# Attention products of a hybrid decoder layer in two float32r parts instead of float32

## The chip, the cores and the metric

The kernel runs on one core of one Trainium2 chip. The metric is the device time of one execution in microseconds (us), here the median of several. In the profile PE is the matrix engine's products, PEld its weight loads, DVE the vector engine, ACT the scalar engine, POOL the GpSimd engine and SP the queue that issues most DMAs.

## The reference, cut to what matters

One decoder layer on 256 tokens, with 16 meta tokens in front (272 positions) and a model width of 2048. A combined input projection feeds two kinds of heads: 8 retention heads (`RH`) and 4 mLSTM heads (`MH`). Their outputs pass a head norm and a gate, then an output projection, then a convolution and a gated feed-forward part of width 5632. The part that is changed here is what each head does between the projections:

```python
# retention, per head and chunk
scores = einsum('bhncd,bhnsd->bhncs', q, k) * decay
intra  = einsum('bhncs,bhnse->bhnce', scores, v)
...
# mLSTM, per head and chunk
P   = einsum('bhncd,bhnsd->bhncs', q, k) * exp(D - m_t[..., None])
num = einsum('bhncs,bhnse->bhnce', P, v) + ...
den = sum(P, axis=-1) + ...
return num / maximum(abs(den), exp(-m_t))[..., None]
```

The recurrence over chunks is exact algebra for one causal attention over all 272 positions, and the kernel computes it in that form.

## The kernel before, in words

Positions lie on the columns. `T` = 272 is the number of positions, `NQ` = 258 the number of query positions that are needed. All large products (input projection `wi`, output projection `wo`, feed-forward `wu` and `wd`) take both operands in two float32r parts, a high part (the value rounded to float32r) and a low part (what is left), and add three products: high by high, high by low, low by high. `load_w` (L123 to L132) loads a half tile of weights, 128x1024, into `wraw`, ACT casts it to `whi` (L129) and DVE subtracts to get `wlo` (L131); there are four `wraw` and five `whi` and `wlo` buffers. `mmk` (L134) issues 16 products with `whi` (L138 with the high part of the activations, L139 with the low part) and then 8 with `wlo` (L141). `project` makes one 128-column tile of a projection out of two half tiles and leaves it in one of four PSUM buffers `mmps`.

The attention of a head has these steps, all in plain float32 on PE:

- `values` (L314) transposes the values on PE (L324), subtracts their mean and writes them to `vpad` in three blocks of key positions (L333, ACT).
- `scores` (L336 on) makes three products, one for each block of 128, 128 and 16 keys: the 258, 144 and 16 queries that see them (L339, L340, L341), weights from `kpad`.
- The scores are multiplied into `ppad` (DVE), and `weigh` (L344 on) makes three products with `vpad` as weights (L347, L348, L349). A retention head weighs once, an mLSTM head twice.
- An mLSTM head also needs row sums: POOL adds the second and third block into `late` (L464, L465), and two products with a matrix of ones add over the keys (L467, L468).
- `variance` (L351 on) makes the head norm: ACT squares and casts, DVE subtracts, two products add up (L359, L360), and `rsqrt_m2` (L160 on) goes over ACT (L164, L165, L167) and DVE (L168, L169). `put_mix` (L363) writes the result to `mixh` and `mixl`.

The loop at L491 projects head i and then attends head i-1, so that one head's attention runs beside the next head's projection. The last retention head's attention runs beside the output projection (L537 on), which starts on the heads that are done: for the first four output tiles the mLSTM half of the weights goes first, and the products that need the last head (`mixh[:, 7]`) come at the end. The order of instructions on each engine is set by a scheduler that places them by its own estimate of times; engines then run them strictly in that order.

At the start, `rstd1` (the first norm) is computed beside the first projections: ACT squares the inputs (L246), DVE adds them (L249, L254), one product adds over the partitions (L256), and `rsqrt_m2` and L258 follow. Until `rstd1` is there no projection tile can leave its PSUM buffer, since each is scaled by it: L420 and L416 (`cx`) are the first to do so. The gates of the mLSTM heads (L274 to L305) are short chains over ACT and DVE on 4 rows, and three small products (L301 to L303) turn one of them, `rA`, into columns.

## Time and profile before

| what | value |
|---|---|
| median of 3 runs | 1242.2 us (1242.07 to 1242.63) |
| time of the profiled execution | 1242.43 us |
| its span (first to last instruction) | 1240.7 us |
| PE busy | 1228.6 us, 99% |
| DVE busy | 810.6 us, 65% |
| ACT busy | 661.1 us, 53% |
| POOL busy | 64.5 us, 5% |
| HBM read | 220.75 MB, 180 GB/s over the span |

A float32 product appears in the trace as two instructions on PE, so a group of 16 such products has a count of 32; a float32r product is one. "Mean ns of one" of a PE instruction runs from its start until its result is out, and overlaps the next one; the distance from start to start is what it costs the engine.

### The profile page before, as it was taken

The numbers are of one execution on the slowest core, as the hardware profiler recorded it, in microseconds if no ns is written. First come the engines' busy times: TensorE is split into PE (matmuls) and PEld (weight loads), VectorE is DVE, ScalarE is ACT, GpSimd is POOL, SyncE is SP. The second block draws the span as 40 slices with busy tenths as digits, with TensorE's granted clock in tenths as the row PEclk, the third lists the DMA queues.
The fourth block names the chain that finished last, engine by engine and source line by source line (L and its number), as shares of the span: only waits on it lengthen the run. The fifth ranks groups of instructions, "written<-read, shape, count | busy, mean of one in ns | idle before, by whom it ended". The sixth has DMA issues, their size and how long they took to land.

```text
span 1240.7 us, 22240 instructions
## 1 busy us (share of the span) xinstructions
PE 1228.6 (99%) x9094; PEld 1176.9 (95%) x9094; DVE 810.6 (65%) x1188; ACT 661.1 (53%) x888; POOL 64.5 (5%) x72
## 2 busy tenths in 40 slices
PE   9999999999999999999999999999999999999996
PEld 9999999999999999999999998888999999998885
DVE  8867777766665766667767664445677677664452
ACT  8756756555556556555555543334555555554441
POOL 0100011111110110000000000000000000000010
PEclk9999999999999999999999999999999999999999
DMA  8764555555553666565555666666665555666552
GB/s 272 253 185 154 160 154 161 176 169 162 175 177 121 220 179 214 165 180 183 186 185 175 186 186 186 186 188 188 185 186 174 186 186 181 182 182 188 186 203 68
DMA packets 63687, 224.30 MB, mean 181 GB/s; under 512 B 7392, under 2 KB 8288, under 8 KB 63456
## 3 DMA queue, kind: packets, MB, share of 16 engines
q1 hardware_dynamic: 62928, 220.11, 57.2%
q0 software_dynamic: 656, 2.76, 0.7%
q8 instruction: 71, 1.16, 0.4%
q14 instruction: 32, 0.26, 0.1%
HBM read 220.75 MB, written 2.10 MB: 180 GB/s over the span
## 4 chain that ended last, share of the span: by engine, by line
PE 97%; DVE 1%; ACT 1%; DMA 1%; issue 0%; SPq 0%; ACTq 0%; DVEq 0%
PE mmps L138 24%; PE mmps L139 24%; PE mmps L141 24%; PE atps L630 7%; PE atps L633 7%; PE atps L629 7%; PE atps L347 1%; PE atps L339 0%; DMA wraw<-in_wi 0%; PE atps L324 0%; DMA hT<-in_xT 0%; PE atps L348 0%; DVE wlo L131 0%; PE atps L569 0%; PE atps L340 0%
## 5 line engine op out<-in xcount | busy, mean ns | idle before, releaser
L129 ACT CAST whi<-wraw 128x1024 fp32r<-128x1024 f32 x404 | 423.1, 1049 | 476.3 <-PE mmps L139 258.0
L131 DVE TENSOR_TENSOR wlo<-wraw,whi 128x1024 fp32r<-128x1024 f32 x404 | 495.2, 1227 | 198.7 <-ACT whi L129 191.2
L139 PE MATMUL mmps<-ul,whi 128*128 128x258 f32 x1408 | 345.8, 283 | 0.0
L138 PE MATMUL mmps<-uh,whi 128*128 128x258 f32 x1408 | 345.7, 282 | 0.0
L138 PEld LDWEIGHTS mmps<-uh,whi 128*128 128x128 f32 x1408 | 266.1, 189 | 0.1
L139 PEld LDWEIGHTS mmps<-ul,whi 128*128 128x128 f32 x1408 | 265.2, 188 | 0.1
L138 PE MATMUL mmps<-xh,whi 128*128 128x272 f32 (+2 forms) x880 | 223.5, 287 | 0.6 <-DVE cx L416 0.6
L139 PE MATMUL mmps<-xl,whi 128*128 128x272 f32 (+2 forms) x880 | 223.2, 287 | 0.0
L141 PE MATMUL mmps<-uh,wlo 128*128 128x258 f32 x1408 | 199.2, 284 | 0.0
L141 PEld LDWEIGHTS mmps<-uh,wlo 128*128 128x128 f32 x1408 | 182.4, 189 | 0.0
L138 PEld LDWEIGHTS mmps<-xh,whi 128*128 128x128 f32 x880 | 165.7, 188 | 0.8 <-ACT whi L129 0.8
L139 PEld LDWEIGHTS mmps<-xl,whi 128*128 128x128 f32 x880 | 166.0, 189 | 0.0
L630 PE MATMUL atps<-whi,ml 128*128 128x512 f32 x352 | 140.0, 398 | 0.0
L629 PE MATMUL atps<-whi,mh 128*128 128x512 f32 x352 | 138.1, 392 | 0.0
L141 PE MATMUL mmps<-xh,wlo 128*128 128x272 f32 (+2 forms) x880 | 129.1, 285 | 0.0
L141 PEld LDWEIGHTS mmps<-xh,wlo 128*128 128x128 f32 x880 | 116.4, 188 | 0.1
L574 DVE TENSOR_TENSOR cu<-mmps,rstd 128x258 f32<-128x258 f32 x88 | 37.5, 426 | 116.3 <-PE mmps L141 116.2
L633 PE MATMUL atps<-wlo,mh 128*128 128x512 f32 x352 | 110.4, 395 | 0.0
L630 PEld LDWEIGHTS atps<-whi,ml 128*128 128x128 f32 x352 | 66.1, 188 | 17.1
L633 PEld LDWEIGHTS atps<-wlo,mh 128*128 128x128 f32 x352 | 66.1, 188 | 15.9
L629 PEld LDWEIGHTS atps<-whi,mh 128*128 128x128 f32 x352 | 66.1, 188 | 14.9
L139 PE MATMUL mmps<-mixl,whi 128*128 128x258 f32 x256 | 63.1, 283 | 0.0
(210 smaller groups left out, 1026.3 us busy)
## 6 DMA issues: line engine op xcount, KB each, us to landing
wraw<-in_wu SPq DMA_DIRECT2D x176, 512.0 KB, 3.5
...
```

The lines of the kernel that those rows point to most:

```text
L129: nc.scalar.copy(hi, raw)
L131: nc.vector.tensor_tensor(out=lo, in0=raw, in1=hi.bitcast(F32), op=ALU.subtract)
L138: nc.tensor.matmul(ps, hi[:, k, :], xh(kk), start=kk == first, stop=False)
L139: nc.tensor.matmul(ps, hi[:, k, :], xl(kk), start=False, stop=False)
L141: nc.tensor.matmul(ps, lo[:, k, :], xh(kk), start=False, stop=kk == last)
L347: nc.tensor.matmul(ps[:, 0:NQ], lhs(0), pT[:, 0:CA], start=True, stop=False)
L574: nc.vector.tensor_tensor(out=u, in0=ps[:, :NQ], in1=rstd2, op=ALU.mult)
L629: nc.tensor.matmul(ps, mh[:, k, rows], hi[:, i, :], start=k == 0, stop=False)
L630: nc.tensor.matmul(ps, ml[:, k, rows], hi[:, i, :], start=False, stop=False)
L633: nc.tensor.matmul(ps, mh[:, k, rows], lo[:, i, :], start=False, stop=k == NHF - 1)
```

## The change

Keys, queries, values and weights of the attention are each split into a high and a low float32r part (`khl`, `vhl`, `phl` and two tiles `qh`, `ql`), by an ACT copy and a DVE subtraction each. `scores` and `weigh` then make three products for each of the three blocks, nine where there were three. The row sums of the mLSTM heads are made by `weigh` with a float32r matrix of ones (`ones_r`), two products a block, six where there were two and two additions on POOL. The pieces of 16 rows that were handled apart are now part of one instruction each. To make room, the squares of the first norm are taken in eight pieces of two instead of four pieces of four (`sum2`), and the gate rows use buffers of `wk`.

```diff
-    kpad = [pa.tile([P, 3 * P], F32, name=f"kpad{i}") for i in range(2)]
-    vpad = pa.tile([P, 3, 2 * P], F32, name="vpad")
-    ppad = pa.tile([P, ABC], F32, name="ppad")
...
+    khl = [[pa.tile([P, 3 * P], F32R, name=f"k{p}{i}") for p in "hl"] for i in range(2)]
+    vhl = [pa.tile([P, 3, 2 * P], F32R, name=f"v{p}") for p in "hl"]
+    phl = [pa.tile([P, ABC], F32R, name=f"p{p}") for p in "hl"]
...
-        sum4 = None
-        for k in range(0, KT, 4):
-
-            sq = rope if k % 8 else sqp.tile([P, 4, T], F32, name="sq" if k else "sum4")
+        sum2 = sqp.tile([P, 2, T], F32, name="sum2")
+        for k in range(0, KT, 2):
+
+            sq = rope[:, k % 4 : k % 4 + 2, :] if k else sum2
             with tc.issue_after(copied.ins):
-                squared = nc.scalar.activation(sq, hT[:, k : k + 4, :], AF.Square)
+                squared = nc.scalar.activation(sq, hT[:, k : k + 2, :], AF.Square)
             if k:
                 with tc.issue_after(parted.ins), tc.high_priority():
-                    nc.vector.tensor_tensor(out=sum4, in0=sum4, in1=sq, op=ALU.add)
...
+                    nc.vector.tensor_tensor(out=sum2, in0=sum2, in1=sq, op=ALU.add)
...
-            nc.tensor.matmul(ms[:, :T], inv_dm, sum4[:, 0, :], start=True, stop=True)
+            nc.tensor.matmul(ms[:, :T], inv_dm, sum2[:, 0, :], start=True, stop=True)
...
+            m = nm[0:n, b : b + 1]
+            nc.scalar.activation(vh[0:n, b, :], where[b], AF.Identity, bias=m)
+            nc.vector.scalar_tensor_tensor(out=vl[0:n, b, :], in0=where[b], scalar=m, in1=vh[0:n, b, :].bitcast(F32), op0=ALU.add, op1=ALU.subtract)
+        return vh, vl
+
+    def split(parts, x):
+        hi, lo = parts
+        nc.scalar.copy(hi, x)
+        nc.vector.tensor_tensor(out=lo, in0=x, in1=hi.bitcast(F32), op=ALU.subtract)
+        return parts
+
+
+    PAIRS = ((0, 0), (0, 1), (1, 0))
+
+    BLOCKS = ((0, 0, CA), (P - T0, CA, AB), (2 * P - T0, AB, ABC))
+
+    def scores(k, q):
 
         ps = at.tile([P, 512], F32, name="atps")
-        nc.tensor.matmul(ps[:, 0:CA], kT[:, 0:P], qT[:, 0:NQ], start=True, stop=True)
-        nc.tensor.matmul(ps[:, CA:AB], kT[:, P : 2 * P], qT[:, P - T0 : NQ], start=True, stop=True)
-        nc.tensor.matmul(ps[:, AB:ABC], kT[:, 2 * P : 3 * P], qT[:, 2 * P - T0 : NQ], start=True, stop=True)
+        for b, (c0, a0, a1) in enumerate(BLOCKS):
+            for i, j in PAIRS:
+                nc.tensor.matmul(ps[:, a0:a1], k[i][:, b * P : (b + 1) * P], q[j][:, c0:], start=i == j, stop=i == 1)
         return ps
 
-    def weigh(lhs, pT):
+    def weigh(lhs, p, pairs=PAIRS):
 
         ps = at.tile([P, 512], F32, name="atps")
-        nc.tensor.matmul(ps[:, 0:NQ], lhs(0), pT[:, 0:CA], start=True, stop=False)
-        nc.tensor.matmul(ps[:, P - T0 : NQ], lhs(1), pT[:, CA:AB], start=False, stop=False)
-        nc.tensor.matmul(ps[:, 2 * P - T0 : NQ], lhs(2), pT[:, AB:ABC], start=False, stop=True)
+        for b, (c0, a0, a1) in enumerate(BLOCKS):
+            for i, j in pairs:
+                nc.tensor.matmul(ps[:, c0:NQ], lhs(i, b), p[j][:, a0:a1], start=b == i == j == 0, stop=b == 2 and (i, j) == pairs[-1])
         return ps
...
+    def k_parts(h, x):
+        split([k[:, :T] for k in khl[h % 2]], x)
+        return khl[h % 2]
+
+    def q_parts(x):
+        return split([wk.tile([P, NQ], F32R, name=f"q{p}") for p in "hl"], x)
...
-        nc.vector.tensor_tensor(out=pT[:, :AB], in0=sps[:, :AB], in1=decay[:, :AB], op=ALU.mult)
-        nc.vector.tensor_tensor(out=pT[0:CC, AB:], in0=sps[0:CC, AB:ABC], in1=decay[0:CC, AB:], op=ALU.mult)
-        o = weigh(lambda b: v[:, b, :], pT)
+        nc.vector.tensor_tensor(out=decay, in0=sps[:, :ABC], in1=decay, op=ALU.mult)
+        o = weigh(lambda i, b: v[i][:, b, :], split(phl, decay))
...
-        late = wk.tile([P, CB], F32, name="late", bufs=1)
-        nc.gpsimd.tensor_tensor(out=late, in0=pT[:, P - T0 : CA], in1=pT[:, CA:AB], op=ALU.add)
-        nc.gpsimd.tensor_tensor(out=late[0:CC, P:], in0=late[0:CC, P:], in1=pT[0:CC, AB:], op=ALU.add)
-        den = at.tile([P, 512], F32, name="atps")
-        nc.tensor.matmul(den[:, 0 : P - T0], ones, pT[:, 0 : P - T0], start=True, stop=True)
-        nc.tensor.matmul(den[:, P - T0 : NQ], ones, late, start=True, stop=True)
+        nc.vector.scalar_tensor_tensor(out=e, in0=sps[:, :ABC], scalar=DK ** -0.5, in1=e, op0=ALU.mult, op1=ALU.mult)
+        p = split(phl, e)
+        den = weigh(lambda i, b: ones_r, p, PAIRS[:2])
```

The scheduler gives the engines another order. Three places matter below.

**First norm, PE.** Here is PE's order around the product of the first norm (`inv_dm`), before. `mmps_510` is the tile of head 0's second values, `mmps_573` the next one, head 0's first gate.

```order
L139 MATMUL mmps_510<-xl_95,whi_543 128x272
L141 MATMUL mmps_510<-xh_94,wlo_545 128x272 x4
L256 MATMUL atps_434<-sum4_423,inv_dm_75 128x272
L141 MATMUL mmps_510<-xh_94,wlo_545 128x272 x4
L139 MATMUL mmps_573<-xl_95,whi_576 128x258
```

After, where `mmps_595` is the first gate and `whi_628` the second half of its weights:

```order
L138 MATMUL mmps_595<-xh_94,whi_628 128x258
L139 MATMUL mmps_595<-xl_95,whi_628 128x258
L138 MATMUL mmps_595<-xh_94,whi_628 128x258
L257 MATMUL atps_449<-sum2_432,inv_dm_75 128x272
L139 MATMUL mmps_595<-xl_95,whi_628 128x258
```

The product has moved back from the values' tile into the second half of the gate's tile: 19 products of that tile are left behind it, where 43 products were left before PE comes to the next tile, which needs a PSUM buffer that is freed only after `rstd1`.

**First norm, DVE.** DVE's order from the norm's product to the buffer that is freed, before; L416 reads `mmps`, the buffer of head 0's queries.

```order
L168 SCALAR_TENSOR_TENSOR rt<-atps,rt 128x272
L169 SCALAR_TENSOR_TENSOR r_436<-rt,r_436 128x272
L258 TENSOR_SCALAR rstd_83<-r_436 128x272
L278 TENSOR_TENSOR g_455<-g_455,rstd_83 4x272
L278 TENSOR_TENSOR qT<-qT,rstd_83 4x272
L420 TENSOR_TENSOR cx<-atps,rstd_83 128x272
L416 TENSOR_TENSOR cx<-mmps,rstd_83 128x262
```

After; L437 is what L416 was:

```order
L168 SCALAR_TENSOR_TENSOR rt<-atps,rt 128x272
L169 SCALAR_TENSOR_TENSOR r_451<-rt,r_451 128x272
L259 TENSOR_SCALAR rstd_83<-r_451 128x272
L131 TENSOR_TENSOR wlo<-wraw,whi 128x1024
L279 TENSOR_TENSOR g_465<-g_465,rstd_83 4x272
L279 TENSOR_TENSOR kq<-kq,rstd_83 4x272
L441 TENSOR_TENSOR cx<-atps,rstd_83 128x272
L437 TENSOR_TENSOR cx<-mmps,rstd_83 128x262
```

One weight subtraction (L131) now stands between `rstd1` and the buffer's release.

**Gate rows, ACT.** ACT's order behind that place in the changed kernel; L281 to L283 make the forget gate's logarithm on 4 rows, from which DVE gets `rA` (now a buffer `e`) by L284, L285 and L286. The columns of `rA` are made by L303 on PE.

```order
L443 ACTIVATE kq<-cx,par 128x272
L456 ACT_TABLE_LOAD
L456 ACTIVATE g_656<-g_656 128x258
L281 ACTIVATE vT_467<-kq 4x272
L282 ACTIVATE vT_468<-vT_467 4x272
L283 ACT_TABLE_LOAD
L283 ACTIVATE vT_468<-vT_468 4x272
```

Before, the same steps were spread out between weight casts, and the products of `rA` (L301) stood later on PE. Now L303 stands on PE 41 products behind the tile that waits for the freed buffer.

**Last retention head, PE.** PE's order around the last product of the last head's variance (`inv_ret`) before, with the four output tiles `mmps_4687` to `mmps_4690`:

```order
L139 MATMUL mmps_4687<-mixl_90,whi_4813 128x258
L360 MATMUL atps_4592<-vl_4589,inv_ret_77 128x258
L138 MATMUL mmps_4687<-mixh_89,whi_4813 128x258
L139 MATMUL mmps_4687<-mixl_90,whi_4813 128x258
L138 MATMUL mmps_4688<-mixh_89,whi_4847 128x258
```

and 41 more such products, on heads that are done, before the first one that needs the last head. After, the four tiles are `mmps_5002` to `mmps_5005`, and the first rows behind L375 are those that need it:

```order
L139 MATMUL mmps_5005<-mixl_90,whi_5234 128x258
L374 MATMUL atps_4907<-vh_4903,inv_ret_77 128x258
L375 MATMUL atps_4907<-vl_4904,inv_ret_77 128x258
L138 MATMUL mmps_5002<-mixh_89,whi_5128 128x258
L138 MATMUL mmps_5003<-mixh_89,whi_5162 128x258
L138 MATMUL mmps_5004<-mixh_89,whi_5198 128x258
L138 MATMUL mmps_5005<-mixh_89,whi_5234 128x258
L139 MATMUL mmps_5002<-mixl_90,whi_5128 128x258
L141 MATMUL mmps_5002<-mixh_89,wlo_5130 128x258 x8
```

Behind L375 no product of another head is left in the changed kernel.

More of the change, by code (lines that the diff above doesn't have):

```diff
@@ L185, in trunk @@
     sel = pa.tile([P, MH * P], F32R, name="sel")
-    kpad = [pa.tile([P, 3 * P], F32, name=f"kpad{i}") for i in range(2)]
-    vpad = pa.tile([P, 3, 2 * P], F32, name="vpad")
-    ppad = pa.tile([P, ABC], F32, name="ppad")
-    for kt in kpad:
-        nc.gpsimd.memset(kt[:, T:], 0.0)
-    nc.gpsimd.memset(vpad[:, 2, :], 0.0)
-    nc.gpsimd.memset(ppad[:, AB:], 0.0)
+    khl = [[pa.tile([P, 3 * P], F32R, name=f"k{p}{i}") for p in "hl"] for i in range(2)]
+    vhl = [pa.tile([P, 3, 2 * P], F32R, name=f"v{p}") for p in "hl"]
+    phl = [pa.tile([P, ABC], F32R, name=f"p{p}") for p in "hl"]
+    for kt in khl[0] + khl[1]:
+        nc.gpsimd.memset(kt[:, T:].bitcast(F32), 0.0)
+    for vt in vhl:
+        nc.gpsimd.memset(vt[:, 2, :].bitcast(F32), 0.0)
+    ones_r = pa.tile([P, P], F32R, name="ones_r")
+    acol = pa.tile([P, 3, MH], F32, name="acol")
+    nc.gpsimd.memset(acol, 0.0)
     wk_cm = pool("wk", 2, side="right")
@@ L239, in trunk @@
         v0_ps = project(next(tiles), xh, xl, 0)
-        sum4 = None
-        for k in range(0, KT, 4):
-            sq = rope if k % 8 else sqp.tile([P, 4, T], F32, name="sq" if k else "sum4")
+        sum2 = sqp.tile([P, 2, T], F32, name="sum2")
+        for k in range(0, KT, 2):
+            sq = rope[:, k % 4 : k % 4 + 2, :] if k else sum2
             with tc.issue_after(copied.ins):
-                squared = nc.scalar.activation(sq, hT[:, k : k + 4, :], AF.Square)
+                squared = nc.scalar.activation(sq, hT[:, k : k + 2, :], AF.Square)
             if k:
                 with tc.issue_after(parted.ins), tc.high_priority():
-                    nc.vector.tensor_tensor(out=sum4, in0=sum4, in1=sq, op=ALU.add)
-            else:
-                sum4 = sq
+                    nc.vector.tensor_tensor(out=sum2, in0=sum2, in1=sq, op=ALU.add)
         with tc.high_priority():
-            for n in (2, 1):
-                nc.vector.tensor_tensor(out=sum4[:, 0:n, :], in0=sum4[:, 0:n, :], in1=sum4[:, n : 2 * n, :], op=ALU.add)
+            nc.vector.tensor_tensor(out=sum2[:, 0, :], in0=sum2[:, 0, :], in1=sum2[:, 1, :], op=ALU.add)
             ms = at.tile([P, 512], F32, name="atps")
-            nc.tensor.matmul(ms[:, :T], inv_dm, sum4[:, 0, :], start=True, stop=True)
+            nc.tensor.matmul(ms[:, :T], inv_dm, sum2[:, 0, :], start=True, stop=True)
             r = rsqrt_m2(wk, ms[:, :T], T, squared)
@@ L267, in trunk @@
         nc.vector.tensor_scalar(out=norms[:, RH:], in0=par[:, a : a + 2 * MH], scalar1=-0.25, scalar2=None, op0=ALU.mult)
-    row = lambda name: pa.tile([MH, T], F32, name=name)
-    rB, rA, rM, rm, rones = map(row, ("rB", "rA", "rM", "rm", "rones"))
-    ri, rf, ra, re = (wk.tile([P, T], F32, name=i)[0:MH, :] for i in ("g0", "qT", "vT0", "vT1"))
+    row = lambda name, **kw: wk.tile([P, T], F32, name=name, **kw)[0:MH, :]
+    ri, rf, ra, re, rB, rA, rM = (row(i) for i in ("g0", "kq", "vT0", "vT1", "g1", "e", "e"))
+    rones, rm = row("hj0", bufs=1), row("hj1", bufs=1)
     bi, bf = par[0:MH, _COLS["bi"][0] : _COLS["bi"][1]], par[0:MH, _COLS["bf"][0] : _COLS["bf"][1]]
@@ L286, in trunk @@
     nc.vector.tensor_tensor_scan(rM, rones, rA, 0.0, op0=ALU.mult, op1=ALU.max)
-    nc.vector.tensor_tensor(out=rm, in0=rB, in1=rM, op=ALU.add)
+    rm = rm[:, :NQ]
+    nc.vector.tensor_tensor(out=rm, in0=rB[:, T0:], in1=rM[:, T0:], op=ALU.add)
     parts = pa.tile([P, 2, NQ], F32R, name="parts")
@@ L291, in trunk @@
         nc.scalar.copy(sel, sel32)
+        nc.scalar.copy(ones_r, ones)
     zero = wk.tile([P, NQ], F32, name="y")
     nc.vector.memset(zero, 0.0)
-    for i, x in enumerate((rM, rm)):
+    for i, x in enumerate((rM[:, T0:], rm)):
         nc.scalar.copy(parts[:, i, :], zero)
         hi, lo = parts[0:MH, i, :], parts[GW // 2 : GW // 2 + MH, i, :]
-        nc.scalar.copy(hi, x[:, T0:])
-        nc.vector.tensor_tensor(out=lo, in0=x[:, T0:], in1=hi.bitcast(F32), op=ALU.subtract)
-    acol = pa.tile([P, 3, MH], F32, name="acol")
+        nc.scalar.copy(hi, x)
+        nc.vector.tensor_tensor(out=lo, in0=x, in1=hi.bitcast(F32), op=ALU.subtract)
     aps = at.tile([P, 512], F32, name="atps")
@@ L330, in values @@
         nc.vector.tensor_scalar(out=nm[0:CC, 2:3], in0=nm[0:CC, 2:3], scalar1=-1.0 / w, scalar2=None, op0=ALU.mult)
-        v = vpad[:, :, 0:w]
+        vh, vl = (v[:, :, 0:w] for v in vhl)
         for b, (s0, n) in enumerate(blocks):
-            nc.scalar.activation(v[0:n, b, :], where[b], AF.Identity, bias=nm[0:n, b : b + 1])
-        return v
-    def scores(kT, qT):
+            m = nm[0:n, b : b + 1]
[4 more added lines that the diff above has]
+        hi, lo = parts
+        nc.scalar.copy(hi, x)
+        nc.vector.tensor_tensor(out=lo, in0=x, in1=hi.bitcast(F32), op=ALU.subtract)
+        return parts
+    PAIRS = ((0, 0), (0, 1), (1, 0))
+    BLOCKS = ((0, 0, CA), (P - T0, CA, AB), (2 * P - T0, AB, ABC))
+    def scores(k, q):
         ps = at.tile([P, 512], F32, name="atps")
-        nc.tensor.matmul(ps[:, 0:CA], kT[:, 0:P], qT[:, 0:NQ], start=True, stop=True)
-        nc.tensor.matmul(ps[:, CA:AB], kT[:, P : 2 * P], qT[:, P - T0 : NQ], start=True, stop=True)
-        nc.tensor.matmul(ps[:, AB:ABC], kT[:, 2 * P : 3 * P], qT[:, 2 * P - T0 : NQ], start=True, stop=True)
+        for b, (c0, a0, a1) in enumerate(BLOCKS):
+            for i, j in PAIRS:
+                nc.tensor.matmul(ps[:, a0:a1], k[i][:, b * P : (b + 1) * P], q[j][:, c0:], start=i == j, stop=i == 1)
         return ps
-    def weigh(lhs, pT):
+    def weigh(lhs, p, pairs=PAIRS):
         ps = at.tile([P, 512], F32, name="atps")
-        nc.tensor.matmul(ps[:, 0:NQ], lhs(0), pT[:, 0:CA], start=True, stop=False)
-        nc.tensor.matmul(ps[:, P - T0 : NQ], lhs(1), pT[:, CA:AB], start=False, stop=False)
-        nc.tensor.matmul(ps[:, 2 * P - T0 : NQ], lhs(2), pT[:, AB:ABC], start=False, stop=True)
+        for b, (c0, a0, a1) in enumerate(BLOCKS):
+            for i, j in pairs:
+                nc.tensor.matmul(ps[:, c0:NQ], lhs(i, b), p[j][:, a0:a1], start=b == i == j == 0, stop=b == 2 and (i, j) == pairs[-1])
         return ps
@@ L365, in put_mix, with rotate @@
         nc.vector.tensor_tensor(out=mixl[:, i, :], in0=y, in1=mixh[:, i, :].bitcast(F32), op=ALU.subtract)
-    def rotate(ps, t0, which, o):
+    def rotate(ps, t0, which):
         n = T - t0
+        o = wk.tile([P, T], F32, name="kq")
         c, s = rope[:, 2 * which, t0:], rope[:, 2 * which + 1, t0:]
@@ L376, in rotate @@
         nc.gpsimd.tensor_tensor(out=o[:, :n], in0=o[:, :n], in1=x[:, :n], op=ALU.add)
-        return o
+        return o[:, :n]
+    def k_parts(h, x):
[3 more added lines that the diff above has]
+        return split([wk.tile([P, NQ], F32R, name=f"q{p}") for p in "hl"], x)
     def ret_project(h):
@@ L381, in ret_project @@
         nc.gpsimd.dma_start(decay, io["decay"][h])
-        kT = rotate(project(next(tiles), xh, xl, 0), 0, 1, kpad[h % 2])
-        qT = rotate(project(next(tiles), xh, xl, T0), T0, 0, wk.tile([P, T], F32, name="qT"))
+        kT = k_parts(h, rotate(project(next(tiles), xh, xl, 0), 0, 1))
+        qT = q_parts(rotate(project(next(tiles), xh, xl, T0), T0, 0))
         vT = scaled(project(next(tiles), xh, xl, 0), 0, "vT0")
@@ L396, in ret_attend @@
         sps = scores(kT, qT)
-        pT = ppad
-        nc.vector.tensor_tensor(out=pT[:, :AB], in0=sps[:, :AB], in1=decay[:, :AB], op=ALU.mult)
-        nc.vector.tensor_tensor(out=pT[0:CC, AB:], in0=sps[0:CC, AB:ABC], in1=decay[0:CC, AB:], op=ALU.mult)
-        o = weigh(lambda b: v[:, b, :], pT)
+        nc.vector.tensor_tensor(out=decay, in0=sps[:, :ABC], in1=decay, op=ALU.mult)
+        o = weigh(lambda i, b: v[i][:, b, :], split(phl, decay))
         s2 = wk.tile([P, NQ], F32, name="s2")
@@ L408, in ret_attend, with conv_silu @@
         put_mix(h, y)
-    def conv_silu(ps, f, t0, o):
+    def conv_silu(ps, f, t0):
         x = wk.tile([P, T + 3], F32, name="cx")
@@ L420, in conv_silu @@
             nc.vector.tensor_tensor(out=x[:, 3:], in0=ps[:, :T], in1=rstd1, op=ALU.mult)
-        kept, o = o, o[:, :n]
+        o = wk.tile([P, T], F32, name="kq")[:, :n]
         nc.scalar.activation(o, x[:, 3 : 3 + n], AF.Identity, scale=pcol("cw", 4 * f + 3), bias=pcol("cb", f))
@@ L425, in conv_silu @@
         nc.scalar.activation(o, o, AF.Silu)
-        return kept
+        return o
     def ml_project(h):
-        kT = conv_silu(k_ps if h == 0 else project(next(tiles), xh, xl, 0), MH + h, 0, kpad[h % 2])
-        qT = conv_silu(q_ps if h == 0 else project(next(tiles), xh, xl, TQ), h, TQ, wk.tile([P, T], F32, name="qT"))
+        kT = k_parts(h, conv_silu(k_ps if h == 0 else project(next(tiles), xh, xl, 0), MH + h, 0))
+        qT = q_parts(conv_silu(q_ps if h == 0 else project(next(tiles), xh, xl, TQ), h, TQ))
         vTs = [scaled(v0_ps if h == j == 0 else project(next(tiles), xh, xl, 0), 0, f"vT{j}") for j in range(2)]
@@ L448, in ml_attend @@
                                        in1=big[:, CA:AB], op0=ALU.subtract, op1=ALU.max)
-        nc.vector.scalar_tensor_tensor(out=e[0:CC, AB:], in0=mps[0:CC, 2 * P - T0 : NQ], scalar=acol[0:CC, 2, h : h + 1],
-                                       in1=big[0:CC, AB:], op0=ALU.subtract, op1=ALU.max)
-        nc.scalar.activation(e[:, :AB], e[:, :AB], AF.Exp, scale=-1.0)
-        nc.scalar.activation(e[0:CC, AB:], e[0:CC, AB:], AF.Exp, scale=-1.0)
+        nc.vector.scalar_tensor_tensor(out=e[:, AB:], in0=mps[:, 2 * P - T0 : NQ], scalar=acol[:, 2, h : h + 1],
+                                       in1=big[:, AB:], op0=ALU.subtract, op1=ALU.max)
+        nc.scalar.activation(e, e, AF.Exp, scale=-1.0)
         m2 = at.tile([P, 512], F32, name="atps")
@@ L457, in ml_attend @@
         sps = scores(kT, qT)
-        pT = ppad
-        sc = DK ** -0.5
-        nc.vector.scalar_tensor_tensor(out=pT[:, :AB], in0=sps[:, :AB], scalar=sc, in1=e[:, :AB], op0=ALU.mult, op1=ALU.mult)
-        nc.vector.scalar_tensor_tensor(out=pT[0:CC, AB:], in0=sps[0:CC, AB:ABC], scalar=sc, in1=e[0:CC, AB:], op0=ALU.mult, op1=ALU.mult)
-        late = wk.tile([P, CB], F32, name="late", bufs=1)
-        nc.gpsimd.tensor_tensor(out=late, in0=pT[:, P - T0 : CA], in1=pT[:, CA:AB], op=ALU.add)
-        nc.gpsimd.tensor_tensor(out=late[0:CC, P:], in0=late[0:CC, P:], in1=pT[0:CC, AB:], op=ALU.add)
-        den = at.tile([P, 512], F32, name="atps")
-        nc.tensor.matmul(den[:, 0 : P - T0], ones, pT[:, 0 : P - T0], start=True, stop=True)
-        nc.tensor.matmul(den[:, P - T0 : NQ], ones, late, start=True, stop=True)
+        nc.vector.scalar_tensor_tensor(out=e, in0=sps[:, :ABC], scalar=DK ** -0.5, in1=e, op0=ALU.mult, op1=ALU.mult)
+        p = split(phl, e)
+        den = weigh(lambda i, b: ones_r, p, PAIRS[:2])
         nc.vector.tensor_tensor(out=floor, in0=den[:, :NQ], in1=floor, op=ALU.max)
@@ L473, in ml_attend @@
         for j in range(2):
-            o = weigh(lambda b: v[:, b, j * P : (j + 1) * P], pT)
+            o = weigh(lambda i, b: v[i][:, b, j * P : (j + 1) * P], p)
             hj = wk.tile([P, NQ], F32, name=f"hj{j}", bufs=1)
```

## The prediction

> **What bounds the kernel now.** First the page: busy times, then the chain that ended last.

> ```profile
> PE 1228.6 (99%) x9094; PEld 1176.9 (95%) x9094; DVE 810.6 (65%) x1188; ACT 661.1 (53%) x888; POOL 64.5 (5%) x72
> ...
> PE 97%; DVE 1%; ACT 1%; DMA 1%; issue 0%; SPq 0%; ACTq 0%; DVEq 0%
> ```

> PE is busy for all but 12 us, mostly at the two ends. So a PE-time difference goes into the result at full size, and so does every wait that PE does not have now. The other engines matter only where they make PE wait. The table by stage shows how far they are from that in the heads' stage:

> ```profile
> 300.00:400.00 100.00, 100.00 (x810) 99.43 (x809) 63.11 (x111) 56.55 (x85) 12.01 (x9) 1.00 0.53 160
> ```

> PE 100 of 100 us, DVE 63, ACT 57.

> **Products.** Counts come from the groups (the last row, the weight subtraction's, serves further down), prices from the timeline of the last head's weighing.

> ```profile
> L347 PE MATMUL atps<-ppad,vpad 128*128 128x258 f32 x32 | 9.7, 385 | 0.0
> L339 PE MATMUL atps<-qT,kpad 128*128 128x258 f32 x24 | 7.3, 386 | 0.2 <-ACT floor L456 0.2
> L131 DVE TENSOR_TENSOR wlo<-wraw,whi 128x1024 fp32r<-128x1024 f32 x404 | 495.2, 1227 | 198.7 <-ACT whi L129 191.2
> ```
> ```profile
> 386.77 0.60 PE L347 MATMUL atps<-ppad,vpad 128*128 128x258 f32 x2
> 387.20 0.41 PE L348 MATMUL atps<-ppad,vpad 128*128 128x144 f32 x2
> 387.45 0.29 PE L349 MATMUL atps<-ppad,vpad 128*128 128x16 f32 x2
> 387.59 0.37 PE L138 MATMUL mmps<-mixh,whi 128*128 128x258 f32 x1
> 387.79 0.29 PE L139 MATMUL mmps<-mixl,whi 128*128 128x258 f32 x1
> ...
> 390.82 1.12 PE L141 MATMUL mmps<-mixh,wlo 128*128 128x258 f32 x8
> 391.78 0.28 PE L138 MATMUL mmps<-mixh,whi 128*128 128x258 f32 x1
> ```

> With two instructions a float32 product there are 16 weighings and 12 scores; the 4 mLSTM heads make 4 row sums. A long float32r product costs (391.78 - 390.82) / 8 = 0.12 us. The float32 group of 258, 144 and 16 columns costs 387.79 - 386.77 = 1.02 us less the 0.12 us of the L138 product in it: 0.90 us (0.43 + 0.25 + 0.14, and 0.08 that the next product is late).

> The new group has nine float32r products: three of 258 columns, three of 144, three of 16. None below 258 columns is in the trace. What it shows is the weight load each needs:

> ```profile
> 387.56 0.19 PEld L138 LDWEIGHTS mmps<-mixh,whi 128*128 128x128 f32 x1
> 387.67 0.19 PEld L139 LDWEIGHTS mmps<-mixl,whi 128*128 128x128 f32 x1
> ```

> Behind the 16-column product, where columns hold nothing up, two float32r loads start 0.11 us apart. So a short product costs 0.11 us however few its columns: the group costs 3 x 0.12 + 6 x 0.11 = 1.02 us, 0.12 us more than now, and 28 groups cost +3.4 us. A row sum has two float32 products, of 144 columns (0.25) and 114 (0.20, by columns): 0.45. Six float32r products take 2 x 0.12 + 4 x 0.11 = 0.68, times four +0.9 us. Products: **+4.3 us**. The bounds: short products priced by columns alone (144 at 0.067, 16 at 0.007) give a group of 0.58, a row sum of 0.39 and -9.2 us in all; a 144-column product priced as float32 (0.25) and a 16-column one at one load give 1.44, 0.96 and +17 us. I take the load rows, since they are float32r loads behind a short product, the case itself.

> [...]

> **Work on ACT and DVE.** Each head gains three ACT copies and some six DVE subtractions; by the rows of L364 and L365 (0.41 and 0.43 us for 258 columns, below) some 1.4 us of ACT and 2.5 us of DVE a head. A retention head has 4 tiles of 48 products, 23 us at 0.12, and some 2 us of attention: 25 us, in which DVE goes from 63% to about 73%. PE's products hide it, and the weight parts are made up to five half tiles ahead; without that cover it would be 30 us over 12 heads. POOL loses `late`, for which PE does not wait now. On SP the load of `rope` moves behind two weight loads; it is first needed by a retention head, over 100 us later. These I put at nothing. The casts' place in the fixed orders costs more, at three points.

> **Wait 1, first norm.**

> ```profile
> 35.82 0.62 PE L256 MATMUL atps<-sum,inv_dm 128*128 128x272 f32 x2
> 37.27 0.48 ACT L164 ACTIVATE r<-atps,epsc 128x272 f32<-128x272 f32 x1
> 39.67 0.30 DVE L258 TENSOR_SCALAR rstd<-r 128x272 f32<-128x272 f32 x1
> ...
> 42.20 0.36 PE L138 MATMUL mmps<-xh,whi 128*128 128x258 f32 x1 [0.58 <-DVE cx L416]
> ```

> Today PE waits 0.58 us here, though 43 products stood behind the norm's product. After, 19 stand there: PE arrives 0.5 (a float32 product, as L347) + 19 x 0.12 = 2.8 us after that product starts. The chain from there: the product 0.62; L164 to the end of L258, 39.97 - 37.27 = 2.7; one L131, 1.2 (its mean above is 1227 ns); then L279 to L437, as today from 39.97 to PE's start at 42.20, 2.2. That is 6.7 us; some 0.6 less if these four instructions take what their like take elsewhere (0.43 each, as L365 below). PE waits 3.3 to 3.9 us, or 2.7 to 3.3 more than now: **+3.1 us**.

> **Wait 2, gate rows.** The columns of `rA` stand 41 products behind that point, 4.9 us. The chain to it now runs on ACT in one piece:

> ```profile
> 43.22 0.61 ACT L422 ACTIVATE kpad<-cx,par 128x272 f32<-128x272 f32 x1
> ...
> 45.61 1.28 ACT L435 ACT_TABLE_LOAD   x1
> 46.91 0.42 ACT L435 ACTIVATE g<-g 128x258 f32<-128x258 f32 x1
> ...
> 53.27 0.71 DVE L284 TENSOR_TENSOR_SCAN rB<-rones,qT 4x272 f32<-4x272 f32 x1
> ...
> 55.02 0.48 DVE L285 SCALAR_TENSOR_TENSOR rA<-g,par,rB 4x272 f32<-4x272 f32 x1
> ```

> 0.61 + two table loads of 1.28 + four ACTIVATEs of 0.42 + DVE's 0.48, 0.71 and 0.48 = 6.5 us. It starts with L441, one step of some 0.4 before the buffer is free: 6.1 behind that point, against 4.9, and back-to-back instructions overlap a little. **+1.1 us**, between 0.5 and 1.7. Weight subtractions queue behind it on DVE, but their half tiles are several ahead.

> **Wait 3, last retention head.**

> ```profile
> 389.49 1.28 ACT L158 ACT_TABLE_LOAD   x1
> ...
> 393.34 0.28 PE L360 MATMUL atps<-vl,inv_ret 128*128 128x258 f32 x1
> 393.66 0.48 ACT L164 ACTIVATE r<-atps,epsc 128x258 f32<-128x258 f32 x1 [1.59 <-PE atps L360]
> 396.98 0.41 ACT L364 CAST mixh<-y 128x258 fp32r<-128x258 f32 x1 [1.94 <-DVE y L407]
> 397.42 0.43 DVE L365 TENSOR_TENSOR mixl<-y,mixh 128x258 fp32r<-128x258 f32 x1 [0.47 <-ACT mixh L364]
> 398.75 0.64 PE L138 MATMUL mmps<-mixh,whi 128*128 128x258 f32 x4
> ```

> From L360 to the end of `mixh` takes 397.39 - 393.34 = 4.05 us today, and PE fills it with 44 products, up to 398.75. After, none is left: weighing is spread among the products that used to fill it, and behind L375 PE meets the products that need `mixh`. Nor does the table load overlap any more: it stands between the cast `vh` and L164. From that cast: 1.28 + (397.39 - 393.66) = 5.0 us, while PE still has 0.6 us (the subtraction and L375). **+4.4 us**, between 4.0 and 4.6.

> **Sum.** 4.3 + 3.1 + 1.1 + 4.4 = 12.9 on the profiled execution's 1242.43: 1255.3. That execution stands 0.2 us above the median of 1242.2, so 1255.1 us for a median.

> **Rivals.** *The clock falls in the long waits.* The end of the trace shows it:

> ```profile
> 1231.00:1234.00 3.00, 0.30 (x2) 0.00 (x0) 1.41 (x4) 1.22 (x4) 1.14 (x1) 1.00 0.33 111
> 1234.00:1237.00 3.00, 0.00 (x0) 0.00 (x0) 1.18 (x4) 1.33 (x2) 0.12 (x1) 0.62 0.44 162
> 1237.00:1241.00 4.00, 0.00 (x0) 0.00 (x0) 0.00 (x0) 0.00 (x0) 0.00 (x0) 0.50 0.44 141
> ```

> PE's last 0.30 us are in the first row, so its last product ends at 1231.3; a mean of 0.62 over 1234 to 1237 means that the granted clock went to half at 1234.7, 3.4 us later. Waits 1 and 3 are 3.3 to 4.6 us, so either may just reach it. If half speed then lasts as long as it took to come, 3.4 us, a fall costs 1.7 to 2.2 us: 1257 for one, 1259 for both. Against it: the waits barely exceed the time. [...]

> *Short float32r products run at float32's rate.* The upper bound above, +17 instead of +4.3: 1268. For it: no float32r product under 258 columns is in the trace. Against: nothing shows a rate that depends on the width.

> *The waits are filled.* If the chains run shorter beside other work than I add up, only products and a part of the waits remain: 1247 to 1249. Against: the orders are strict, and the 0.58 us of L416 is there already.

> *Not slower: short products cost their columns.* Place: the 184 short products that replace float32's; price: -9.2 us, which with the waits' 8.6 gives 1241.6. It decides from a group price of 0.69 us, where 28 x 0.21 and the waits leave 2.5 us: below it the result cannot be told from before. With 144 columns at 0.067 that is a load of 0.043 us for the 16. Against: 0.11 in the rows. [...]

> **Numbers.** My forecast 0.45, clock 0.25, float32's rate 0.17, waits filled 0.08, columns 0.05. 0.2% of this kernel, 2.5 us, is about what its measurement can tell from no change. Faster by more: 0.01, the last case with shorter waits; within: 0.04, the rest of it; slower: 0.95. The range 1250 to 1269 leaves out the last two cases and some of the edges, under 2 in 10.

> **What would show it.** PE busy 4 us higher; in PE's waits one of 3 to 4 us on DVE's `cx` at 42 us, one near 50 us on `rA`'s columns, and one above 4 us on ACT's `mixh` near 410 us; short products 0.11 us apart. The forecast is wrong if PE's idle time does not grow by some 8 us, or if a 144-column product takes 0.2 us or more.

## The result and the profile after

| | before | after |
|---|---|---|
| median of 4 runs | 1242.41 us | 1260.28 us (1259.76 to 1262.06) |
| ratio, 95% interval | | 1.0145 (1.0132 to 1.0157) |
| profiled execution | 1242.43 us, span 1240.7 | 1260.76 us, span 1259.0 |

17.9 us slower in the medians, 18.3 between the two profiled executions, against a forecast of 12.9. The busy times of the changed kernel, from its page:

```profile
PE 1238.6 (98%) x9186; PEld 1188.2 (94%) x9186; DVE 834.1 (66%) x1251; ACT 677.4 (54%) x924; POOL 61.3 (5%) x67
```

PE is busy 10.0 us longer, in a span that is 18.3 us longer: 8.3 us are new idle time. The table of waits of the changed kernel, called after from here on (who waited for whom: time in us, how often, the longest), says where:

```profile
PE mmps L138 <- DVE cx L437: 5.1, 1, 5.1
PE mmps L138 <- ACT mixh L379: 4.3, 1, 4.3
```

Wait 1 and wait 3 are there; wait 2 is not. The table by stage of after (the stretch in us from the start, its length, busy time of PE, PEld, DVE, ACT and POOL with the number of instructions; then the granted clock, that is the share of its full clock that PE was given; then the DMA's share and GB/s) shows what becomes of about half of PE's other 10 us:

```profile
41.38:44.79 3.41, 0.45 (x4) 0.25 (x3) 3.22 (x6) 1.35 (x2) 1.68 (x1) 1.00 0.89 268
44.79:51.62 6.83, 4.73 (x22) 4.76 (x23) 4.97 (x12) 5.07 (x8) 2.71 (x5) 0.50 0.31 110
...
409.99:413.43 3.44, 0.15 (x1) 0.00 (x0) 1.31 (x3) 1.87 (x4) 0.00 (x0) 1.00 0.00 0
413.43:420.26 6.83, 5.85 (x27) 5.85 (x28) 3.15 (x7) 3.71 (x6) 0.00 (x0) 0.50 0.03 7
...
300.00:400.00 100.00, 100.00 (x826) 99.90 (x825) 70.74 (x129) 59.91 (x88) 12.35 (x10) 1.00 0.58 171
```

Behind each of the two waits PE works for some us at half clock: 4.73 us behind the first, 5.85 us behind the second. The last row is the heads' stage: PE full, DVE at 71 of 100 us, where it was 63. The timeline of PE in after, at the two waits (start and duration in us, engine, line, what was done; in brackets the idle time before it and what ended it):

```profile
38.92 0.62 PE L257 MATMUL atps<-sum,inv_dm 128*128 128x272 f32 x2
...
46.89 0.55 PE L138 MATMUL mmps<-xh,whi 128*128 128x258 f32 x1 [5.06 <-DVE cx L437]
...
47.46 0.42 PE L138 MATMUL mmps<-xh,whi 128*128 128x258 f32 x1
...
47.89 0.42 PE L138 MATMUL mmps<-xh,whi 128*128 128x258 f32 x1
...
409.76 0.39 PE L375 MATMUL atps<-vl,inv_ret 128*128 128x258 f32 x1
414.41 1.23 PE L138 MATMUL mmps<-mixh,whi 128*128 128x258 f32 x4 [4.27 <-ACT mixh L379]
```

From 47.46 to 47.89 two products take 0.43 us, 0.215 each instead of 0.12. So a stretch of t us at half clock does the work of 0.56 t: the first costs 4.73 x 0.44 = 2.1 us, the second 5.85 x 0.44 = 2.6 us.

**The account of the 18.3 us.** Wait 1 5.06 less the 0.58 of before: 4.5. Its half-clock stretch: 2.1. Wait 3: 4.3. Its half-clock stretch: 2.6. Products: 4.2 (from the experiment cover, below). Together 17.7. At the very start PE waits 0.4 us for its first weights where it waited 0.9 in before (0.4 to 1.6 in the profiles here), so 17.2 of 18.3 are accounted for and 1.1 us is not assigned.

### The profile page after: what moved, and what is told of

The parts are those of the page before. It is cut to its first block, busy times and chain, and to the rows that moved or that the text cites. A ratio compares the mean times of both kernels' runs of the same rounds, so it can differ in the third digit from the quotient of the medians.

```text
span 1259.0 us, 22504 instructions
## 1 busy us (share of the span) xinstructions
PE 1238.6 (98%) x9186; PEld 1188.2 (94%) x9186; DVE 834.1 (66%) x1251; ACT 677.4 (54%) x924; POOL 61.3 (5%) x67
## 3 DMA queue, kind: packets, MB, share of 16 engines
q8 instruction: 72, 1.18, 0.4%
## 4 chain that ended last, share of the span: by engine, by line
PE 96%; ACT 1%; DMA 1%; DVE 1%; issue 0%; SPq 0%; ACTq 0%; DVEq 0%
PE mmps L138 24%; PE mmps L141 24%; PE mmps L139 24%; PE atps L642 7%; PE atps L645 7%; PE atps L641 6%; PE atps L364 1%; PE atps L356 1%; DMA wraw<-in_wi 0%; PE atps L326 0%; DMA wraw<-in_w 0%; PE atps L581 0%; ACT whi L129 0%; DVE wlo L131 0%; ACT L158 0%
## 5 line engine op out<-in xcount | busy, mean ns | idle before, releaser
L129 ACT CAST whi<-wraw 128x1024 fp32r<-128x1024 f32 x404 | 423.2, 1049 | 442.5 <-PE mmps L139 233.8
L131 DVE TENSOR_TENSOR wlo<-wraw,whi 128x1024 fp32r<-128x1024 f32 x404 | 495.6, 1227 | 195.3 <-ACT whi L129 184.8
L139 PE MATMUL mmps<-ul,whi 128*128 128x258 f32 x1408 | 345.8, 283 | 0.0
L138 PE MATMUL mmps<-uh,whi 128*128 128x258 f32 x1408 | 345.8, 282 | 0.0
L138 PEld LDWEIGHTS mmps<-uh,whi 128*128 128x128 f32 x1408 | 266.1, 189 | 0.1
L139 PEld LDWEIGHTS mmps<-ul,whi 128*128 128x128 f32 x1408 | 265.1, 188 | 0.1
L138 PE MATMUL mmps<-xh,whi 128*128 128x272 f32 (+2 forms) x880 | 225.9, 289 | 5.1 <-DVE cx L437 5.1
L139 PE MATMUL mmps<-xl,whi 128*128 128x272 f32 (+2 forms) x880 | 224.7, 287 | 0.0
L141 PE MATMUL mmps<-uh,wlo 128*128 128x258 f32 x1408 | 199.2, 284 | 0.0
L141 PEld LDWEIGHTS mmps<-uh,wlo 128*128 128x128 f32 x1408 | 182.4, 189 | 0.0
L138 PEld LDWEIGHTS mmps<-xh,whi 128*128 128x128 f32 x880 | 166.9, 190 | 5.3 <-issue 5.2
L139 PEld LDWEIGHTS mmps<-xl,whi 128*128 128x128 f32 x880 | 166.9, 190 | 0.0
L141 PE MATMUL mmps<-xh,wlo 128*128 128x272 f32 (+2 forms) x880 | 132.9, 287 | 0.0
L141 PEld LDWEIGHTS mmps<-xh,wlo 128*128 128x128 f32 x880 | 118.8, 189 | 0.0
L138 PE MATMUL mmps<-mixh,whi 128*128 128x258 f32 x256 | 63.3, 286 | 4.3 <-ACT mixh L379 4.3
```

What stands on the lines that cost most here:

```text
L129: nc.scalar.copy(hi, raw)
L131: nc.vector.tensor_tensor(out=lo, in0=raw, in1=hi.bitcast(F32), op=ALU.subtract)
L138: nc.tensor.matmul(ps, hi[:, k, :], xh(kk), start=kk == first, stop=False)
L139: nc.tensor.matmul(ps, hi[:, k, :], xl(kk), start=False, stop=False)
L141: nc.tensor.matmul(ps, lo[:, k, :], xh(kk), start=False, stop=kk == last)
```

## The experiments

Two theories. **Waits**: most of the loss is two places where PE's order leaves too little work behind a chain, and the clock falls that these waits bring; the products themselves cost some 4 us. **Work**: the added products, casts and subtractions cost the time all over the heads, and the waits are only where it comes to light, so that filling one moves it elsewhere. Beside them a side theory: the half-clock stretches have nothing to do with the waits.

### Wait 1 taken away: q_in_at

```
-    gates_ps, k_ps = (at.tile([P, 512], F32, name="atps") for _ in range(2))
-    q_ps = mm.tile([P, 512], F32, name="mmps")
+    gates_ps, k_ps, q_ps = (at.tile([P, 512], F32, name="atps") for _ in range(3))
```

> Head 0's query accumulator takes a buffer of the other PSUM pool, so 48 more products stand behind the first norm before PE needs a freed buffer. Waits theory: the 5.06 us wait on cx goes, and with it the stretch at half clock behind it (2.1 us): 1253.1 us; 1254.2 if the columns of rA then wait 1.1 us as forecast. Clock on its own (the half-clock stretch has nothing to do with the wait): 1255.2. Work theory (the time comes from the added products and casts, and the wait is only where it shows): within 1 us of 1260.3.

Measured: 1253.30 us (1253.27 to 1253.38), ratio to before 1.0088 (1.0073 to 1.0103): 7.0 us less than the changed kernel. The table of waits of this run has one long wait left, and its table by stage full clock where it was half:

```profile
PE mmps L138 <- ACT mixh L378: 4.3, 1, 4.3
```
```profile
41.70:46.60 4.90, 4.90 (x44) 4.90 (x43) 4.82 (x9) 2.43 (x4) 4.02 (x4) 1.00 0.91 300
46.60:51.60 5.00, 5.00 (x43) 5.00 (x42) 4.62 (x7) 4.96 (x8) 2.04 (x1) 1.00 0.42 131
```

The wait and its stretch went together, and nothing took their place. Work is refuted for this part, and so is a clock that falls on its own. In this kernel the columns of `rA` also moved back on PE, so it says nothing on wait 2.

### One part of the change alone: sums_alone

```
-        sum4 = None
-        for k in range(0, KT, 4):
-
-            sq = rope if k % 8 else sqp.tile([P, 4, T], F32, name="sq" if k else "sum4")
+        sum2 = sqp.tile([P, 2, T], F32, name="sum2")
+        for k in range(0, KT, 2):
+
+            sq = rope[:, k % 4 : k % 4 + 2, :] if k else sum2
...
-            for n in (2, 1):
-                nc.vector.tensor_tensor(out=sum4[:, 0:n, :], in0=sum4[:, 0:n, :], in1=sum4[:, n : 2 * n, :], op=ALU.add)
+            nc.vector.tensor_tensor(out=sum2[:, 0, :], in0=sum2[:, 0, :], in1=sum2[:, 1, :], op=ALU.add)
```

> The kernel before with one part of the change alone: the squares of the first norm are added two tiles at a time instead of four, in seven additions instead of three; float32 attention, rows and pads as before. Its order has the norm's product 19 products before the buffer and one weight subtraction behind rstd1, as in the changed kernel. Waits theory: wait 1 of 4 to 5 us and the fall behind it come with this part alone: 1242.4 + 6.6 = 1249 us. Work theory: the float32r attention makes the cost, so within 1 us of 1242.4.

Measured: 1248.61 us (1248.14 to 1249.18), ratio 1.0052 (1.0038 to 1.0065): 6.4 us slower than before, with all attention in float32. The timelines of DVE and PE of this run, and its table by stage:

```profile
42.79 1.23 DVE L131 TENSOR_TENSOR wlo<-wraw,whi 128x1024 fp32r<-128x1024 f32 x1
```
```profile
46.67 0.55 PE L138 MATMUL mmps<-xh,whi 128*128 128x258 f32 x1 [5.07 <-DVE cx L413]
```
```profile
45.05:51.87 6.82, 5.20 (x24) 5.23 (x25) 5.26 (x13) 5.56 (x9) 2.23 (x4) 0.50 0.30 97
```

The same wait to 0.01 us, the same weight subtraction in the chain, a half-clock stretch of the same length. About a third of the change's cost comes from a part of it that alters no product of the attention: the way the first norm's squares are added up.

### Wait 3 made shorter: lo_first, both, cover

The edit of lo_first, in the first group of output tiles (`cut` is 7 in the half that holds the retention heads):

```
+        for part in (ks,) if cut is None else (ks[:cut], ks[cut:]):
+            mmk(ps, w, part, ...)
```

> In the first four output tiles the 28 weight-remainder products (L141) of finished heads move ahead of the products that need the last retention head: 28 x 0.12 = 3.4 us more cover in its chain. Waits theory: the 4.27 us wait on mixh falls to some 0.9 us, too short for the clock to fall (3.1 us): 1253.8 us. Clock on its own: 1256.9. Work theory: within 1 us of 1260.3.

Measured: 1258.41 us (1257.69 to 1259.21), ratio 1.0129 (1.0114 to 1.0144): 1.9 us less than the changed kernel where 6.5 were expected. The two intervals overlap, though all four executions lie below all four of the changed kernel. The timelines of PE and ACT, and the table by stage, of lo_first:

```profile
411.58 0.28 PE L377 MATMUL atps<-vl,inv_ret 128*128 128x258 f32 x1
...
411.82 0.99 PE L141 MATMUL mmps<-mixh,wlo 128*128 128x258 f32 x7
415.75 1.05 PE L138 MATMUL mmps<-mixh,whi 128*128 128x258 f32 x4 [2.95 <-ACT mixh L381]
```
```profile
411.90 0.48 ACT L166 ACTIVATE r<-atps,epsc 128x258 f32<-128x258 f32 x1 [1.94 <-PE atps L377]
```
```profile
412.58:415.99 3.41, 0.46 (x4) 0.26 (x4) 2.02 (x5) 1.07 (x3) 0.00 (x0) 1.00 0.00 0
415.99:419.40 3.41, 3.41 (x18) 3.41 (x18) 2.29 (x6) 2.35 (x3) 0.00 (x0) 0.50 0.00 0
```

The products did move, but 21 of the 28 to before the variance's last product (L377, the changed kernel's L375). ACT was ready for the variance and waited 1.94 us for it: of 3.4 us of cover 1.94 delayed the chain itself, and the wait shrank by 1.3 us to 2.95. That was still enough: at the end of this shorter wait the clock fell, for 3.41 us.

> Both edits. Waits theory: what is left above the kernel before is the products, 4.2 us, less its 0.58 us wait and plus at most 0.9: 1246 to 1247.5 us, granted clock 1.00 in all stages of the heads. Clock on its own: 1251. Work theory: within 2 us of 1260.3.

Both edits together: 1250.84 us (1249.08 to 1251.10), ratio 1.0063 (1.0046 to 1.0080). The two gains add up (7.0 + 1.9 = 8.9 expected from the single runs, 9.4 measured); the number written down was missed by the same 2.95 us wait (2.94 here) and the same stretch of 3.42 us at half clock.

In cover, which has both edits, the 28 products are also held back until the variance's last product has been issued:

```
-        for k, kk in ks:
-            nc.tensor.matmul(ps, lo[:, k, :], xh(kk), start=False, stop=kk == last)
+        with tc.issue_after(behind.ins) if behind else ExitStack():
+            for k, kk in ks:
+                nc.tensor.matmul(ps, lo[:, k, :], xh(kk), start=False, stop=kk == last)
...
+        last_var = nc.tensor.matmul(var[:, :NQ], mean, lo, start=False, stop=True)
```

> As both, but the 28 weight-remainder products are now held back until behind the last variance product (in lo_first 8 of them and some others had moved ahead of it and delayed it). Cover 28 x 0.12 = 3.4 us in a wait of 4.27: 0.9 us of wait left, clock 1.00 from 50 us to the end of the products. Waits theory: the kernel before, plus 4.0 us of products, less its 0.58 us wait, plus 0.9: 1246.8 us. Work theory (products and casts cost more than that): 1250 or more.

Measured: 1247.16 us (1247.11 to 1247.80), ratio 1.0041 (1.0027 to 1.0055), 0.4 us from what was written. (The expectation speaks of 8 products that had moved ahead in lo_first; its timeline has 21.) Its page and its table of waits:

```profile
PE 1232.8 (99%) x9186; PEld 1182.4 (95%) x9186; DVE 833.3 (67%) x1251; ACT 676.9 (54%) x924; POOL 64.4 (5%) x67
```
```profile
PE mmps L138 <- ACT mixh L382: 0.9, 1, 0.9
```

Of the 17.9 us, 13.1 go with the order of a few products and one PSUM buffer, while every added product, cast and subtraction is still there. As the clock is full up to the last product (0.998 in the mean of the span, in cover as in before), PE's busy time can be compared with before: 1232.8 - 1228.6 = 4.2 us. That is what the products cost.

### Does the wait bring the half clock? filler

```
+        if fill:
+            spare = at.tile([P, 512], F32, name="atps")
+            with tc.issue_after(done.ins), tc.high_priority():
+                for _ in range(fill):
+                    nc.tensor.matmul(spare[:, :NQ], mean, hi, start=True, stop=True)
...
+        r = variance(s2, inv_ret, 30 if h == RH - 1 else 0)
```

> The changed kernel with 30 more float32r products of 258 columns on PE behind L375, whose result nobody reads: 30 x 0.12 = 3.6 us of PE work inside the 4.27 us wait. If the clock falls because PE idles in that wait, it stays at 1.00 behind it and the time falls by 3.1 us to 1257.2 although PE does more. If the clock falls for another reason, 1260.3; if PE's work decides, 1263.9.

Measured: 1258.49 us (1256.68 to 1259.01), ratio 1.0127 (1.0112 to 1.0142): 1.8 us less than the changed kernel, for 30 products more. Here too the intervals overlap, and all four executions lie below all four of the changed kernel. PE's timeline and the table by stage of filler:

```profile
410.31 3.77 PE L380 MATMUL atps<-vh,inv_ret 128*128 128x258 f32 x30
414.75 0.74 PE L138 MATMUL mmps<-mixh,whi 128*128 128x258 f32 x4 [0.66 <-ACT mixh L384]
```
```profile
414.40:420.30 5.90, 5.55 (x46) 5.55 (x47) 4.11 (x8) 4.91 (x9) 0.05 (x1) 1.00 0.17 34
```

The wait's end stands where it stood in after (414.75 against 414.41), but the clock stays at 1.00 and the tiles behind it run at full speed. The mean granted clock says the same of all executions: 0.995 to 0.996 in filler's four, 0.992 to 0.994 in the changed kernel's four. So the idle PE brings the fall. The gain came out at 1.8 us between the medians and 2.2 between the profiled executions, instead of 3.1. The 3.1 was too high: the stretch is worth 2.6 us by the account above, and in this execution PE comes to L375 0.3 us later than in after (410.09 against 409.76), for reasons that lie ahead of the filler.

### The price of a short product: four

Cover with a fourth product in each block:

```
-    PAIRS = ((0, 0), (0, 1), (1, 0))
+    PAIRS = ((0, 0), (0, 1), (1, 0), (1, 1))
...
```

> cover with a fourth product a block, remainder times remainder: 28 groups get one product more of 258, 144 and 16 columns each. If a short product costs a weight load (0.11 us): 28 x (0.12 + 0.11 + 0.11) = 9.5 us more than cover. If it costs its columns: 28 x (0.12 + 0.067 + 0.007) = 5.4 us more. If short float32r products ran at float32's rate (0.25 for 144 columns): 13.4 us more. The longer stream may also fill the 0.9 us that cover still waits; that is read from its profile.

Measured: 1255.70 us (1255.48 to 1256.01), ratio 1.0109 (1.0094 to 1.0125): 8.5 us more than cover, 9.4 with cover's 0.9 us wait, which is filled here. The page of four:

```profile
PE 1241.6 (99%) x9270; PEld 1191.5 (95%) x9270; DVE 836.1 (67%) x1251; ACT 674.5 (54%) x922; POOL 64.1 (5%) x67
```

84 instructions more take 1241.6 - 1232.8 = 8.8 us of PE, 0.105 us each. A weight load a product (9.5) is confirmed within a tenth; columns alone (5.4) and float32's rate (13.4) are out. With 0.12 us for the 28 wide ones, 0.097 us are left for a short product.

### A version that beats both: wide_only, and q_before

Three products of 258 columns take 0.36 us where the float32 one took 0.43; three of 144 or of 16, at 0.10 us each, take more than the float32 one they replace (0.30 against 0.25, and against 0.14). wide_only is cover with float32r parts in the wide block alone:

```
-        for b, (c0, a0, a1) in enumerate(BLOCKS):
-            for i, j in PAIRS:
-                nc.tensor.matmul(ps[:, a0:a1], k[i][:, b * P : (b + 1) * P], q[j][:, c0:], start=i == j, stop=i == 1)
+        for i, j in PAIRS:
+            nc.tensor.matmul(ps[:, 0:CA], k[0][i], q[0][j], start=i == j, stop=i == 1)
+        for b in (1, 2):
+            c0, a0, a1 = BLOCKS[b]
+            nc.tensor.matmul(ps[:, a0:a1], k[1][:, (b - 1) * P : b * P], q[1][:, c0:], start=True, stop=True)
```

and likewise in `weigh`.

> cover, but only the block of 258 columns takes its operands in two float32r parts; the blocks of 144 and 16 columns are float32 products again (from k, v, p and q kept in float32). By the rows: 3 x 0.12 = 0.36 instead of 0.43 us in 28 groups, -2.0; the four row sums 2 x 0.12 + 0.25 + 0.14 instead of 0.45, +0.7; the kernel before's 0.58 us wait gone. 1240.5 us, if the waits theory holds and no new wait comes up: 0.15% faster than before. Work theory: 1246 or more.

Measured over 11 runs: 1240.06 us (1239.72 to 1241.51), ratio to before 0.9982 (0.9973 to 0.9990). Its page and PE's timeline at one group of scores:

```profile
PE 1227.0 (99%) x9130; PEld 1177.5 (95%) x9130; DVE 824.6 (67%) x1227; ACT 674.3 (54%) x935; POOL 63.4 (5%) x64
```
```profile
382.16 0.28 PE L359 MATMUL atps<-qh,kl 128*128 128x258 f32 x1
382.28 0.54 PE L362 MATMUL atps<-q,k 128*128 128x144 f32 x4
382.67 0.37 PE L384 MATMUL atps<-vl,inv_ret 128*128 128x258 f32 x1
```

1227.0 - 1228.6 = -1.6 us of PE, where -1.3 was worked out, and no long wait. The last run takes away the same wait of before without new products: before with q_in_at's edit and nothing else.

> The kernel before with head 0's query accumulator in the other PSUM pool, nothing else: its 0.58 us wait on cx goes. 1241.7 us, within 0.2% of before. If wide_only's gain of 2.2 us came from this edit and not from its products, 1240.

Measured over 11 runs: 1241.62 us (1241.46 to 1242.27), ratio 0.9994 (0.9985 to 1.0003): its interval holds 1. The 0.58 us wait is gone from its profile, and its gain is too small to tell from none; wide_only's is not. The two intervals overlap (0.9985 to 0.9990), so the times alone part the edit from the products only weakly. PE's busy time, in one execution of each, agrees with the products: 1227.0 us in wide_only, 1228.6 in before, whose products q_before has too.

## Why the prediction was right, and where its sizes were off

The direction and the mechanism held: two order waits and dearer short products, 1250 to 1269 forecast, 1260.28 measured. But the likeliest case was not the one that came. What came is the first rival, the clock falling behind both waits, which had 0.25 and 1259 us. PE's idle time grew by 8.3 us, close to the 8.6 of the three waits, but partly by luck: one wait came out longer and another did not come.

**Products, +4.3: measured 4.2.** The row of loads 0.11 us apart was the right one to take. The group of scores in after's timeline:

```profile
398.20 0.28 PE L356 MATMUL atps<-qh,kl 128*128 128x258 f32 x1
398.32 0.23 PE L356 MATMUL atps<-qh,kh 128*128 128x144 f32 x1
398.39 0.27 PE L356 MATMUL atps<-ql,kh 128*128 128x144 f32 x1
398.50 0.27 PE L356 MATMUL atps<-qh,kl 128*128 128x144 f32 x1
398.61 0.22 PE L356 MATMUL atps<-qh,kh 128*128 128x16 f32 x1
398.68 0.26 PE L356 MATMUL atps<-ql,kh 128*128 128x16 f32 x1
398.80 0.37 PE L375 MATMUL atps<-vl,inv_ret 128*128 128x258 f32 x1
```

Starts lie 0.07 to 0.12 us apart, whether a product has 144 columns or 16. From 398.32 to 398.80 that is 0.10 us each, a little under the load's 0.11; behind the group the next wide product takes 0.20 instead of 0.12 us (399.03 to 399.23), which the prediction had counted for the float32 group (its 0.08) but not for the new one. The two nearly cancel, so that the sum came out this close is in part luck. Work on ACT and DVE at nothing: right, DVE went to 71 of 100 us (73 forecast) and cover shows no wait for it in the heads.

**Wait 1, +3.1: measured 4.5. The term was mis-sized, in its chain.** The timelines of ACT and DVE in after:

```profile
39.32 1.05 ACT L129 CAST whi<-wraw 128x1024 fp32r<-128x1024 f32 x1 [0.23 <-DMA wraw<-in_wi]
40.28 0.48 ACT L164 ACTIVATE r<-atps,epsc 128x272 f32<-128x272 f32 x1
```
```profile
42.67 0.30 DVE L259 TENSOR_SCALAR rstd<-r 128x272 f32<-128x272 f32 x1
43.01 1.23 DVE L131 TENSOR_TENSOR wlo<-wraw,whi 128x1024 fp32r<-128x1024 f32 x1
44.15 1.00 DVE L279 TENSOR_TENSOR g<-g,rstd 4x272 f32<-4x272 f32 x1
45.07 0.98 DVE L279 TENSOR_TENSOR kq<-kq,rstd 4x272 f32<-4x272 f32 x1
...
46.34 0.41 DVE L437 TENSOR_TENSOR cx<-mmps,rstd 128x262 f32<-128x262 f32 x1
```

The prediction gave the norm's product 0.62 us up to L164. Here it is 40.28 - 38.92 = 1.36, and the rows that it quoted of before had it as well: 37.27 - 35.82 = 1.45. The product is not what takes longer. On ACT a weight cast (L129) stands ahead of L164 and ends only as L164 starts, in after by the row above and in before by this one:

```profile
36.32 1.05 ACT L129 CAST whi<-wraw 128x1024 fp32r<-128x1024 f32 x1 [0.65 <-DMA wraw<-in_wi]
```

Where ACT is free, L164 starts 0.04 us behind the end of the product it reads (the prediction's rows of the last head: 393.34 + 0.28 and 393.66). So the chain left out what ACT still had to do, and came out 0.7 us short; no run took the cast away. From L164 to the end of `rstd1` 2.7 us and the subtraction 1.2 us came as forecast. From the first L279 to PE's restart it takes 46.89 - 44.15 = 2.7 us; 2.2 was forecast as the upper value, and "some 0.6 less" was allowed for. The two L279 take 1.00 and 0.98 us; their like in before (L278) took 0.43 and 1.00.

**Wait 2, +1.1: it did not come.** The rows of its two ends, from DVE's timeline and from the view of one source line (the starts are behind the durations), in after:

```profile
52.56 0.49 DVE L286 SCALAR_TENSOR_TENSOR e<-g,par,g 4x272 f32<-4x272 f32 x1
```
```profile
L303 PE MATMUL atps<-ident,e x2: 247/258/268, 54.1 to 54.2; 4*128 4x4 f32 x2
```

`rA` is done at 53.05, 6.2 us behind PE's restart at 46.89, where 6.1 was forecast: the chain was right. But PE comes to the columns at 54.1, 1.05 us later still. The half clock had held PE up by 2.1 us on the way; by these numbers it would have waited some 1.05 us at full clock. That is an estimate: no kernel here ran this order at full clock.

**Wait 3, +4.4: measured 4.3.** The chain with the table load in it, and no product behind L375, as read from the order.

**The clock.** Priced at 1.7 to 2.2 us a fall, it cost 2.1 and 2.6. The chance was the step that failed: 0.25, with waits of 3.3 to 4.6 us held against the 3.4 us that the end of the trace shows. Those 3.4 us come from one place, and in the runs less was enough: a wait of 2.95 us in lo_first, and in after the 3.41 us ahead of the first fall still have 0.45 us of PE in them (41.38 to 44.79). Behind seven of the eight waits of 2.9 us or more the rows show a fall, with the clock at 0.50 or wide products 0.21 to 0.22 us apart: 5.06 and 4.27 us in after, 5.07 in sums_alone, 4.65 and 2.95 in lo_first, 2.94 in both and 4.36 in filler (its wait at the first norm). Behind the eighth, 4.3 us in q_in_at, no row here shows the clock; that execution's mean of 0.995 is that of filler with its one fall, against 0.998 in cover.

**Sum.** 12.9 forecast. Wait 1 +1.4, wait 2 -1.1, products and wait 3 -0.2, two clock falls +4.7, together 17.7; less the 0.5 at the start, 17.2 of 18.3.
